# First stage of a hybrid decoder layer: loads on GpSimd's queue, stores on SP's, a fourth store tile, and a different order at both ends of the stage

## The chip, the cores and the metric

One core of a Trainium2 chip runs the kernel. Time is the device time of one execution in microseconds (us), and the figure to predict is the median of the runs. TensorE multiplies matrices (PE in the profile, PEld its weight loads), VectorE (DVE) and ScalarE (ACT) work on tiles, GpSimd (POOL) does some element-wise work and can issue DMAs, and SyncE (SP) only issues DMAs. Each of these engines takes its instructions strictly in the order in which the program gives them; a DMA issue that has to wait holds everything behind it in its engine's queue.

## The reference

```python
def reference(x, norm_gain, w_in, ret_gn_gain, w_out, final_gain):
    h = rms_norm(x, norm_gain[0])                 # x: (1, 4096, 1024) float32
    x = x + hybrid_mixer(h, w_in[0], ret_gn_gain[0], w_out[0])
    return rms_norm(x, final_gain)

def hybrid_mixer(h, w_in, ret_gn_gain, w_out):
    qa, ka, va, ga, qr, kr, vr, gr = split(h @ w_in, IN_SPLITS)   # 512 x4, 256 x2, 512 x2
    attn = dilated_attention(qa, ka, va)   # 8 heads x 64, rotary, three (window, dilation) branches
    ret = retention(qr, kr, vr)            # 4 heads, key 64, value 128, rotary, chunks of 128
    mixed = [silu(ga) * attn, silu(gr) * ret * ret_gn_gain]
    return mixed @ w_out
```

The first stage of the kernel computes the queries, keys and values: `rms_norm(x)` times the columns of `w_in` for `qa`, `ka`, `va`, `qr` and `kr`, with the rotary positions applied, and stores them in DRAM.

## The kernel before

Three stages follow each other: `phase1` (projections), `phase2` (the attention branches, the retention and `vr`'s projection), `phase3` (gates and output projection). The change is in `phase1` and in what it prepares for `phase2`.

`phase1` goes over the 4096 positions twice, in blocks q of 512 positions: q = 0 to 7 give the keys (bank 0, stored to `dr_k`) and the retention's rows (bank 1, to `dr_r`); q = 8 to 15 give the queries (`dr_q`) and the values (bank 1, `dr_v`). Every float32 product is three products of split operands (hi times hi, hi times lo, lo times hi). In place of eight 2x2 block products there are seven, P1 to P7 (`PRODUCTS`), of sums and differences of the four quarters of a block's input; each is done for two banks. So a block has 14 steps, and a step is 24 matmuls of 128x256 (L390). The quarters are the tiles `xt` (128x4x256), loaded by `load_x` (L284), changed in place by `sum_t` (L297), and split by `hi_x` (ACT, L305) and `lo_x` (DVE, L309) into `h`. Each block's sums of squares come from a second, untransposed load `xn` (`load_n`, L316; `square`, L323 on ACT; one tile for `xn` and `diag` together); `root` (L328 DVE, L330 and L332 POOL), `along_free` (PE, L341) and `copy_rb` make the row `rb` of 1/rms, with which `scale_table` (POOL, L362) scales the cosine and sine tables `tab` (`load_table`, L358).

Results leave PSUM by `snapshot` (ACT, L411 and L409) and `join` (DVE, L426 and L422) and are rotated on DVE (`rotate`, L470 to L475). Everything that is stored passes through one pool, `hlp`, tag `hl`, with three buffers: the two split key or query tiles of a half block (`hi_o` L502 or L500, `lo_o` L510 or L508, `store_o` L516), the retention's tile `or` of a half (`store_r` L484), the value tiles `vo` (`store_values`, L440 and L443 on SP and L447 on POOL).

A hand-written table sets the order: `at(step, fn, ...)` puts a function behind the matmuls of that step, with s = 14q. The final loop goes through the steps, and each engine gets its instructions in that order. Lines that matter here:

```python
hlp = pool("p1hl", 3)
at(s + 10, rotate, q, 0, 1)      # keys or queries, half 1
at(s + 12, hi_o, q, 1)
at(s + 14, store_o, q, 1)
at(s + 16, hi_o, q, 0)
at(s + 19, store_o, q, 0)
at(s + 15, rotate, q, 1, 0)      # q < 8: retention's tile "or", half 0
at(s + 17, rotate, q, 1, 1)      #        and half 1
at(s + 17, store_r, q, 0)
at(s + 18, store_r, q, 1)
at(s + 12, store_values, q, 1)   # q >= 8
```

SP issues all loads and all stores but L447. Between q = 7 and q = 8 the weights for the second pass are loaded (`load_raw`) and combined. At the end of the stage the first tiles of `phase2` are prepared: its keys (`first_k`), weights `w2` (`w2_load`, L74; `w2_split`, L83 on ACT and L84 on DVE), a chunk of x (`first_chunk`, L783; `first_chunk_split`, L792 on DVE and L795 on POOL) and queries (`first_q`, L900); the first matmuls of `phase2` are `V` (L48 to L50), of that chunk and `w2`.

Of the kernel before, what the change touches and what calls it, by code (L numbers as in the profile page):

```python
# [27 lines left out]
BLK = 512  # L28
# [110 lines left out]
def phase1(tc, io, dr, right, ahead):  # L139
# [5 lines left out]
    with ExitStack() as ctx:  # L145
# [1 line left out]
            return ctx.enter_context(tc.tile_pool(name=name, bufs=bufs, **kw))  # L147

        wp = pool("p1w", 1)
        rawp = pool("p1x", 6)  # L150
        hp = pool("p1h", 3)
        sm = pool("p1s", 2)
        tp = pool("p1t", 1)
        op = pool("p1o", 2)
        hlp = pool("p1hl", 3)
        mp = pool("p1m", 7)
        pyz = pool("p1y", 2, space=PSUM)
        pss = pool("p1ss", 1, space=PSUM)
# [14 lines left out]
        ident = wp.tile([128, 128], F32, name="ident1")  # L173
        make_identity(nc, ident)

        def whole(p, tag):
            return lambda dt: (lambda t: [t[:, k, :] for k in range(4)])(p.tile([128, 4, 512], dt, tag=tag, name=f"w1{tag}"))

        def pieces(p, tags, n):
            def get(dt):  # L180
                ts = [p.tile([128, n, 512], dt, tag=tag, name=f"w1{tag}") for tag in tags]
                return [ts[k // n][:, k % n, :] for k in range(4)]

            return get
# [33 lines left out]
            },  # L218
        )

        def load_w(ps, dst, part, k):

            rows = io["w1"][k * 128 : (k + 1) * 128, :]

            def pairs_of(c0):
                return rows[:, c0 : c0 + 512].rearrange("k (u t c) -> k t u c", t=2, c=128)[:, part]

            nc.sync.dma_start(dst[:, 0:256].rearrange("k (u c) -> k u c", c=128), pairs_of(0 if ps else 512))
            if ps == 0:
                nc.sync.dma_start(dst[:, 256:512].rearrange("k (u c) -> k u c", c=128), pairs_of(1024))  # L230
            else:
                nc.sync.dma_start(dst[:, 256:512], rows[:, 1536 + 256 * part : 1792 + 256 * part])

# [43 lines left out]
        def load_x(q, part, half, k=None):  # L277

            c0 = q % NBLK * BLK + half * HALF
            if (q, part, half) not in xq:  # L280
                xq[q, part, half] = rawp.tile([128, 4, HALF], F32, tag="x", name="xt1")
            t = xq[q, part, half]
            if k is None:
                nc.sync.dma_start(t, by_blocks(io["xT"])[:, 4 * part : 4 * part + 4, c0 : c0 + HALF])  # L284
            else:
                nc.sync.dma_start(t[:, k, :], io["xT"][(4 * part + k) * 128 : (4 * part + k + 1) * 128, c0 : c0 + HALF])

# [25 lines left out]
        def load_n(q, i):  # L313
            xn[q, i] = tp.tile([128, D], F32, tag="xn", name="xn1")
            n = 4 * q + i
            nc.sync.dma_start(xn[q, i], io["x"][n * 128 : (n + 1) * 128, :])  # L316

        def square(q, i):

# [29 lines left out]

        def load_rb(q):  # L350
            rb = rbs[q] = tp.tile([128, BLK], F32, tag="rb", name="rb1")
            nc.sync.dma_start(rb, dr["rs"][q % NBLK : q % NBLK + 1].rearrange("o i p -> o (i p)").broadcast_to([128, BLK]))

        def load_table(q, n, half):
            c0 = q % NBLK * BLK + half * HALF
            tab = tabs[q, n, half] = tp.tile([128, 2, HALF], F32, tag=f"tab{n}{half}", name="tab1")
            for i, nm in enumerate((f"cos{n}", f"sin{n}")):
                nc.sync.dma_start(tab[:, i, :], io[nm][:, c0 : c0 + HALF].unsqueeze(0).broadcast_to([4, 32, HALF]))  # L358

        def scale_table(q, n, half):  # L360
            rb = rbs[q][:, half * HALF : (half + 1) * HALF].unsqueeze(1).broadcast_to([128, 2, HALF])
# [173 lines left out]
        for q in range(NB2):  # L535
            s = STEPS * q
            one = q < NBLK
            if q:

                for n, (part, half) in zip((12, 10, 8, 5), ((0, 0), (0, 1), (1, 1), (1, 0))):  # L540
                    at(s - n, load_x, q, part, half)
                at(s - 4, hi_x, q, "P1")
                at(s - 3, lo_x, q, "P1")
                at(s - 3, sum_t, q, 1)
                at(s - 2, hi_x, q, "P5")
                at(s, lo_x, q, "P5")
                at(s, sum_t, q, 2)
                at(s + 1, hi_x, q, "P6")
                at(s + 2, lo_x, q, "P6")
            if one and q:  # L550

                a, d = {1: (-3, 2), 2: (-7, 2), 3: (-10, 2)}.get(q, (-14, 3))
                for i in range(4):
                    at(s + a + d * i, load_n, q, i)
                    at(s + a + d * i + d - 1, square, q, i)
                e = s + a + 4 * d
                at(e, root, q)
                at(e + 1, along_free, q)
                at(e + 1, copy_rb, q)
            elif not one:  # L560
                at(s - 2, load_rb, q)
# [15 lines left out]
                    at(s + max(c, {0: 10, 1: 8}.get(q, 0)), scale_table, q, n, half)  # L577

            for bank in range(2):
                at(s + 1 + 2 * bank, snapshot, q, "x", bank, "m1", 0)  # L580
                at(s + 5, snapshot, q, "z", bank, "m5", 1)
# [12 lines left out]
            if one:  # L594
                at(s + 15, rotate, q, 1, 0)
                at(s + 17, rotate, q, 1, 1)
                at(s + 17, store_r, q, 0)
                at(s + 18, store_r, q, 1)
            else:
                at(s + 12, store_values, q, 1)  # L600
                at(s + 14, last_v, q)
                at(s + 15, store_values, q, 0)

# [1 line left out]
        raw = {}  # L605

        def load_raw(name, room, part, k0):
            raw[name] = ROOM[room](F32)
            for k in range(4):
                load_w(1, raw[name][k], part, k0 + k)  # L610

        def diff_d():
            raw["D"] = ROOM["q01"](F32)
# [49 lines left out]

        def w2_load():
            ahead["w2"] = Split(nc, wpool, "w2", io["w2"], scale=gain, tag="w")
            ahead["w2"].load(mp.tile([128, 512], F32, tag="m", name="raw1"))
# [45 lines left out]
        for k in range(4):  # L712
            split_w(0, "P1", Aa, 0, ks=[k])
            hi_x(0, "P1", slice(k, k + 1))
            lo_x(0, "P1", slice(k, k + 1))
            for bank in range(2):
                product(W[0], 0, "P1", bank, [k])
        sum_t(0, 1)
        hi_x(0, "P5")
        lo_x(0, "P5")  # L720
        for k in range(4):
# [3 lines left out]
            split_w(0, "P5", Ba, ks=[k])  # L725
            for bank in range(2):
                product(W[0], 0, "P5", bank, [k])
        sum_t(0, 2)
        hi_x(0, "P6")
        lo_x(0, "P6")  # L730
# [1091 lines left out]
```

## Time and profile before

| | |
|---|---|
| runs | median 2569.85 us of 3, from 2562.11 to 2574.93 |
| the profiled execution | 2571.75 us, of which the span of the profile is 2570.0 |
| stage 1 on TensorE | from 6.63 us to the wait that ends at 916.57 |
| TensorE, 950 to 1000 us (second stage) | busy 50.00 of 50.00, clock 1.00 |
| DMA traffic, 0 to 900 us | 147.25 MB, 137.17 MB of it in SP's queue |

A row of the timeline is start, duration, engine, line, operation, tile written <- tiles read, and in brackets the idle time before it and what ended that. "SPq" is a DMA issue on SP. A row of the waits is waiting engine and line <- what it waited for: total, times, longest. A row of the windows gives, for a stretch of time, the busy time and instructions of each engine, then TensorE's granted clock, the DMA engines' share and GB/s.

### The profile page before, as it was taken

Reading aid. Unit: us, or ns where it says so; the run is one execution under the profiler, and the core shown is the slowest. Engines: PE = TensorE matmul, PEld = TensorE weight load, DVE = VectorE, ACT = ScalarE, POOL = GpSimd, SP = SyncE. Lnnn points to the kernel's source line nnn. Section 1 sums busy time; section 2 is a strip of 40 time slices with the busy share of each in tenths; the row PEclk is TensorE's granted clock in tenths of the full one; section 3 lists DMA queues with packets and bytes.
Section 4 is the critical chain, followed back from the end, with each engine's and each line's share of the span. In section 5 each row is a group of like instructions: output and inputs, shape, how many; then the busy total and the mean of one; then the engine's idle time right before and its main releaser. Section 6 shows DMA issues by size and latency. Waiting matters only on the chain. (4 is left out here: it accounts for less than half of the span.)

```text
span 2570.0 us, 47422 instructions
## 1 busy us (share of the span) xinstructions
PE 2319.0 (90%) x16808; PEld 2086.2 (81%) x16808; DVE 1758.1 (68%) x4221; ACT 1116.3 (43%) x3036; POOL 751.9 (29%) x853
## 2 busy tenths in 40 slices
PE   5768878579999659999999999999799999999998
PEld 5768778579999648888888888787688999999997
DVE  6756777686676547778787787978665656555563
ACT  5333333233232226667667666666532323222231
POOL 1211111312222235444353443544521211212110
PEclk8888988789999879999999999999899999999999
DMA  6444445446666855857658576575576556566563
GB/s 188 145 131 147 144 136 163 136 152 186 184 186 184 208 153 134 192 135 167 160 134 194 129 177 154 129 176 155 155 183 153 162 157 151 161 143 172 143 150 93
DMA packets 480174, 404.93 MB, mean 158 GB/s; under 512 B 197720, under 2 KB 444632, under 8 KB 474816
## 3 DMA queue, kind: packets, MB, share of 16 engines
q1 hardware_dynamic: 472976, 391.64, 57.7%
q0 software_dynamic: 6672, 9.99, 1.5%
q8 instruction: 133, 2.18, 0.4%
q14 instruction: 105, 0.86, 0.1%
q10 hardware_dynamic: 288, 0.26, 0.0%
HBM read 283.12 MB, written 118.64 MB: 156 GB/s over the span
## 5 line engine op out<-in xcount | busy, mean ns | idle before, releaser
L1048 DVE CUSTOM_DVE_ANT_0 S<-S,mask 128x256 f32<-128x256 f32 (+1 forms) x768 | 308.5, 402 | 165.7 <-PE S L1027 131.1
L1055 ACT ACTIVATE P<-S,nm 128x256 f32<-128x256 f32 (+1 forms) x768 | 337.9, 449 | 44.4 <-DVE nm L1048 41.5
L50 PE MATMUL g<-h,wg 128*128 128x256 f32 x1024 | 289.3, 283 | 0.0
L305 ACT ACTIVATE h<-xt 128x1024 fp32r<-128x1024 f32 (+1 forms) x115 | 118.9, 1034 | 225.8 <-DVE xt L297 99.2
L1064 PE MATMUL T<-ident,P 128*128 128x128 f32 x1368 | 214.1, 274 | 0.0
L49 PE MATMUL po<-wo,m 128*128 128x512 f32 x512 | 200.8, 392 | 0.0
L1097 PE MATMUL O<-pt,v 128*64 128x128 f32 (+1 forms) x1968 | 196.5, 326 | 0.0
L50 PEld LDWEIGHTS g<-h,wg 128*128 128x128 f32 x1024 | 195.8, 191 | 0.0
L1027 PE MATMUL S<-kk,qc 128*128 128x256 f32 x1024 | 187.4, 307 | 6.8 <-issue 2.9
L309 DVE TENSOR_TENSOR h<-xt,h 128x1024 fp32r<-128x1024 f32 (+1 forms) x115 | 155.3, 1355 | 52.1 <-ACT h L305 50.4
L48 PE MATMUL po<-wohi,m 128*128 128x512 f32 x448 | 178.7, 399 | 7.2 <-ACT m L40 6.6
L1027 PEld LDWEIGHTS S<-kk,qc 128*128 128x128 f32 x1024 | 150.1, 191 | 35.1 <-issue 17.6
L50 PE MATMUL po<-wohi,m 128*128 128x512 f32 x448 | 177.5, 397 | 0.2 <-DVE m L41 0.2
L1611 POOL TENSOR_TENSOR rs<-v,mhalf 128x1 f32<-128x1 f32 x32 | 17.6, 550 | 547.2 <-DVE v L1609 492.9
L1097 PEld LDWEIGHTS O<-pt,v 128*64 128x64 f32 x1968 | 121.4, 137 | 60.7 <-issue 31.8
L362 POOL TENSOR_TENSOR tab<-tab,rb 128x512 f32<-128x512 f32 x48 | 70.6, 1475 | 339.3 <-DMA tab<-in_sinR_dram 155.7
L1064 PEld LDWEIGHTS T<-ident,P 128*128 128x128 f32 x1368 | 164.6, 142 | 0.2 <-ACT wg0hi L87 0.2
L1550 ACT ACTIVATE e<-g 128x256 f32<-128x256 f32 x128 | 48.3, 379 | 252.9 <-PE g L50 236.4
L795 POOL TENSOR_TENSOR hc<-hr,hc 128x512 fp32r<-128x512 f32 x64 | 85.7, 1339 | 246.2 <-ACT hc L794 180.7
L1055 ACT ACTIVATION_READ_ACCUMULATOR P<-S,nm 128x1 f32 x768 | 157.5, 205 | 0.0
L48 PE MATMUL V<-w2hi,hc 128*128 128x512 f32 x256 | 118.9, 464 | 37.5 <-DVE hc L792 36.7
L49 PE MATMUL g<-h,wg1hi 128*128 128x256 f32 x512 | 145.7, 285 | 1.9 <-DVE h L843 1.8
(267 smaller groups left out, 6511.4 us busy)
## 6 DMA issues: line engine op xcount, KB each, us to landing
hr<-in_xT_dram SPq DMA_DIRECT2D x64, 512.0 KB
q<-dr_q SPq DMA_DIRECT2D x128, 256.0 KB
xt<-in_xT_dram SPq DMA_DIRECT2D x63, 512.0 KB
wb<-dr_w SPq DMA_DIRECT2D x128, 192.0 KB
o<-dr_o SPq DMA_DIRECT2D x192, 128.0 KB
v<-dr_v SPq DMA_DIRECT2D x94, 256.0 KB
xn<-in_x_dram SPq DMA_DIRECT2D x32, 512.0 KB
dr_k<-hl SPq DMA_DIRECT2D x64, 256.0 KB
```

Of the source, the lines that this page charges most:

```text
L48: nc.tensor.matmul(out, wh, xh, start=first and i == 0, stop=False)
L49: nc.tensor.matmul(out, wh, xl, start=False, stop=False)
L50: nc.tensor.matmul(out, wl, xh, start=False, stop=last and i == n - 1)
L305: nc.scalar.activation(xs[q, prod][:, 0, ks, :], xq[(q, *SOURCE[prod])][:, ks, :], AF.Copy)
L309: (engine or nc.vector).tensor_tensor(h[:, 1, ks, :], src[:, ks, :], f32(h[:, 0, ks, :]), ALU.subtract)
L362: nc.gpsimd.tensor_tensor(tabs[q, n, half], tabs[q, n, half], rb, ALU.mult)
L795: nc.gpsimd.tensor_tensor(hc[:, :, 1, :], src, hc[:, :, 0, :].bitcast(F32), ALU.subtract)
L1027: nc.tensor.matmul(s[:, j * 256 : (j + 1) * 256], qq[h, t, half][:, off : off + 128] if br == 0 else it["q"][:, t, i, :], rhs, start=(j == ...
L1048: nc.vector.tensor_tensor_reduce(sv, sv, mask[:, it["br"], c0:256], 1.0, BIG, ALU.add, ALU.min, accum_out=nm[:, col : col + 1])
L1055: nc.scalar.activation(it["P", i // 2][:, i % 2, c0:256], sv, AF.Exp, bias=nm[:, col : col + 1], scale=-1.0, accum_out=den[:, col : col + 1])
L1064: nc.tensor.transpose(t[:, j * 128 : (j + 1) * 128], it["P", bank][:, j // 2, j % 2 * 128 : j % 2 * 128 + 128], ident)
L1097: nc.tensor.matmul(o[64 * bank : 64 * bank + 64, c0 : c0 + 128 * m], vt[h, br, idx // 8][:, idx % 8, :], it["pt"][:, a : a + m, :].rearran ...
```

## The change

- `load_x` for q > 0, `load_n`, `load_table`, `load_rb` and the first keys of `phase2` are issued by GpSimd's queue; the startup's loads of x and weights, and all stores that were SP's, stay on SP.
- `hlp` gets four buffers. The six shared buffers of `xt` become five: two for the quarter (0,0), one each for the others; the order and steps in which the quarters are loaded change with it.
- `load_raw` fetches the last 256 columns of its weights in one or two DMAs in place of four.
- The squares of blocks 5 to 7 move two steps earlier; block 0's snapshots are issued right behind the products they copy, ahead of the work for the next product.
- `store_values` of half 1 moves from step s+12 to s+11. At the end, `w2` is loaded in four lots over four steps, `w2_split` and the first chunk move by one step, and `first_q` from s-4 to s.

The diff, cut to its core:

```diff
-        rawp = pool("p1x", 6)
+        rawp = pool("p1x", 1)
+        raw2p = pool("p1x2", 2)
-        hlp = pool("p1hl", 3)
+        hlp = pool("p1hl", 4)
...
             if (q, part, half) not in xq:
-                xq[q, part, half] = rawp.tile([128, 4, HALF], F32, tag="x", name="xt1")
+                p = rawp if part or half else raw2p
+                xq[q, part, half] = p.tile([128, 4, HALF], F32, tag=f"x{part}{half}", name="xt1")
             if k is None:
-                nc.sync.dma_start(t, by_blocks(io["xT"])[:, 4 * part : 4 * part + 4, c0 : c0 + HALF])
+                (nc.gpsimd if q else nc.sync).dma_start(t, by_blocks(io["xT"])[:, 4 * part : 4 * part + 4, c0 : c0 + HALF])
...
-            nc.sync.dma_start(xn[q, i], io["x"][n * 128 : (n + 1) * 128, :])
+            nc.gpsimd.dma_start(xn[q, i], io["x"][n * 128 : (n + 1) * 128, :])
...
-                nc.sync.dma_start(tab[:, i, :], io[nm][:, c0 : c0 + HALF].unsqueeze(0).broadcast_to([4, 32, HALF]))
+                nc.gpsimd.dma_start(tab[:, i, :], io[nm][:, c0 : c0 + HALF].unsqueeze(0).broadcast_to([4, 32, HALF]))
...
-                for n, (part, half) in zip((12, 10, 8, 5), ((0, 0), (0, 1), (1, 1), (1, 0))):
+                for n, (part, half) in zip((12, 10, 8, 6), ((0, 0), (1, 1), (0, 1), (1, 0))):
...
-                a, d = {1: (-3, 2), 2: (-7, 2), 3: (-10, 2)}.get(q, (-14, 3))
+                a, d = {1: (-3, 2), 2: (-7, 2), 3: (-10, 2), 4: (-14, 3)}.get(q, (-16, 3))
...
-                at(s + 12, store_values, q, 1)
+                at(s + 11, store_values, q, 1)
...
-        at(s - 12, load_raw, "Aa", "wh0", 0, 0)
+        at(s - 11, load_raw, "Aa", "wh0", 0, 0)
-        at(s - 10, load_raw, "Ab", "p40", 0, 4)
+        at(s - 8, load_raw, "Ab", "p40", 0, 4)
...
-            ahead["kk"] = load_k(nc, kka, dr, 0)
+            ahead["kk"] = load_k(nc, kka, dr, 0, nc.gpsimd.dma_start)
...
-        at(s - 6, first_chunk)
-        at(s - 4, first_q)
         for i in range(4):
-            at(s - 4 + i, w2_split, (2 * i, 2 * i + 1))
-        at(s - 1, first_chunk_split)
+            at(s - 8 + i, w2_some, (2 * i, 2 * i + 1))
+        at(s - 5, first_chunk)
+        at(s, first_q)
+        for i in range(4):
+            at(s - 3 + i, w2_split, (2 * i, 2 * i + 1))
+        at(s - 2, first_chunk_split)
...
+        for bank in range(2):
+            snapshot(0, "x", bank, "m1", 0)
```

SP's queue in block 4, before (`dr_rs` is the row of 1/rms that `copy_rb` stores; a number behind a tile's name tells one buffer's use from the next):

```order
L346 DMA dr_rs<-rb_2262 1x512
L358 DMA tab_2265<-in_cosA_dram 128x1x256
L358 DMA tab_2265<-in_sinA_dram 128x1x256
L516 DMA dr_k<-hl_2214 128x2x256 x2
L516 DMA dr_k<-hl_2215 128x2x256 x2
L316 DMA xn_2299<-in_x_dram 128x1024
L358 DMA tab_2371<-in_cosA_dram 128x1x256
L358 DMA tab_2371<-in_sinA_dram 128x1x256
L284 DMA xt_2374<-in_xT_dram 128x4x256
L484 DMA dr_r<-or_2326 4x32x256 x4
L316 DMA xn_2420<-in_x_dram 128x1024
L484 DMA dr_r<-or_2403 4x32x256 x4
```

The same stretch of SP's queue now:

```order
L353 DMA dr_rs<-rb_2267 1x512
L523 DMA dr_k<-hl_2217 128x2x256 x2
L523 DMA dr_k<-hl_2218 128x2x256 x2
L491 DMA dr_r<-or_2331 4x32x256 x4
L491 DMA dr_r<-or_2408 4x32x256 x4
L523 DMA dr_k<-hl_2371 128x2x256 x2
L523 DMA dr_k<-hl_2372 128x2x256 x2
```

The loads are gone from between the stores. They stand in POOL's queue, among its own work (L369 is `scale_table`), which before held `scale_table` and `root` alone:

```order
L323 DMA xn_2344<-in_x_dram 128x1024
L365 DMA tab_2378<-in_cosA_dram 128x1x256
L365 DMA tab_2378<-in_sinA_dram 128x1x256
L291 DMA xt_2381<-in_xT_dram 128x4x256
L369 TENSOR_TENSOR tab_2270<-tab_2270,rb_2267 128x512
L365 DMA tab_2458<-in_cosR_dram 128x1x256
L365 DMA tab_2458<-in_sinR_dram 128x1x256
L291 DMA xt_2461<-in_xT_dram 128x4x256
L323 DMA xn_2463<-in_x_dram 128x1024
L369 TENSOR_TENSOR tab_2378<-tab_2378,rb_2267 128x512
```

A multiply of a table now stands between the loads, and each table's load is four steps ahead of its multiply, as before.

The end of the stage in SP's queue, before (`w` and `raw` are the rows of `w2`, `hr` the chunk of x, `vo` the values of block 15, half 1):

```order
L74 DMA w_7956<-in_w_dram 128x512
L74 DMA raw_7943<-in_w_dram 128x512
L783 DMA hr_8017<-in_xT_dram 128x8x128
L900 DMA q_00_8081<-dr_q 32x2048 x4
L900 DMA q_10_8086<-dr_q 32x2048 x4
L440 DMA dr_v<-vo_8014 8x16x512
L443 DMA dr_v<-vo_8014 8x16x512
L440 DMA dr_v<-vo_8014 8x16x512
L443 DMA dr_v<-vo_8014 8x16x512
```

And now:

```order
L74 DMA w_8032<-in_w_dram 128x512
L74 DMA raw_7935<-in_w_dram 128x512
L807 DMA hr_8035<-in_xT_dram 128x8x128
L447 DMA dr_v<-vo_7999 8x16x512
L450 DMA dr_v<-vo_7999 8x16x512
L447 DMA dr_v<-vo_7999 8x16x512
L450 DMA dr_v<-vo_7999 8x16x512
L1746 DMA rgain_8270<-in_ret_gain_dram 128x4
L807 DMA hr_8160<-in_xT_dram 128x8x128
L523 DMA dr_q<-hl_8144 128x2x256 x2
L523 DMA dr_q<-hl_8145 128x2x256 x2
L924 DMA q_00_8209<-dr_q 32x2048 x4
```

The values' stores have changed places with the loads of the queries.

More of the change, by code (lines that the diff above doesn't have):

```diff
@@ L174, in phase1, with get @@
         make_identity(nc, ident)
+        WHOLE = {}
         def whole(p, tag):
-            return lambda dt: (lambda t: [t[:, k, :] for k in range(4)])(p.tile([128, 4, 512], dt, tag=tag, name=f"w1{tag}"))
+            def get(dt):
+                t = WHOLE[tag] = p.tile([128, 4, 512], dt, tag=tag, name=f"w1{tag}")
+                return [t[:, k, :] for k in range(4)]
+            return get
         def pieces(p, tags, n):
             def get(dt):
-                ts = [p.tile([128, n, 512], dt, tag=tag, name=f"w1{tag}") for tag in tags]
+                ts = WHOLE["h0"] = [p.tile([128, n, 512], dt, tag=tag, name=f"w1{tag}") for tag in tags]
                 return [ts[k // n][:, k % n, :] for k in range(4)]
@@ L219, in phase1, with pairs_of @@
         )
+        def pairs_of(rows, c0, part):
+            return rows[:, c0 : c0 + 512].rearrange("k (u t c) -> k t u c", t=2, c=128)[:, part]
         def load_w(ps, dst, part, k):
             rows = io["w1"][k * 128 : (k + 1) * 128, :]
-            def pairs_of(c0):
-                return rows[:, c0 : c0 + 512].rearrange("k (u t c) -> k t u c", t=2, c=128)[:, part]
-            nc.sync.dma_start(dst[:, 0:256].rearrange("k (u c) -> k u c", c=128), pairs_of(0 if ps else 512))
+            nc.sync.dma_start(dst[:, 0:256].rearrange("k (u c) -> k u c", c=128), pairs_of(rows, 0 if ps else 512, part))
             if ps == 0:
-                nc.sync.dma_start(dst[:, 256:512].rearrange("k (u c) -> k u c", c=128), pairs_of(1024))
+                nc.sync.dma_start(dst[:, 256:512].rearrange("k (u c) -> k u c", c=128), pairs_of(rows, 1024, part))
             else:
@@ L351, in load_rb @@
             rb = rbs[q] = tp.tile([128, BLK], F32, tag="rb", name="rb1")
-            nc.sync.dma_start(rb, dr["rs"][q % NBLK : q % NBLK + 1].rearrange("o i p -> o (i p)").broadcast_to([128, BLK]))
+            nc.gpsimd.dma_start(rb, dr["rs"][q % NBLK : q % NBLK + 1].rearrange("o i p -> o (i p)").broadcast_to([128, BLK]))
         def load_table(q, n, half):
@@ L579, in phase1 @@
             for bank in range(2):
-                at(s + 1 + 2 * bank, snapshot, q, "x", bank, "m1", 0)
-                at(s + 5, snapshot, q, "z", bank, "m5", 1)
+                if q:
+                    at(s + 1 + 2 * bank, snapshot, q, "x", bank, "m1", 0)
+                    at(s + 5, snapshot, q, "z", bank, "m5", 1)
                 at(s + 6 + bank, snapshot, q, "x", bank, "u2", 1)
@@ L607, in load_raw @@
         def load_raw(name, room, part, k0):
-            raw[name] = ROOM[room](F32)
+            raw[name] = t = ROOM[room](F32)
             for k in range(4):
-                load_w(1, raw[name][k], part, k0 + k)
+                rows = io["w1"][(k0 + k) * 128 : (k0 + k + 1) * 128, :]
+                nc.sync.dma_start(t[k][:, 0:256].rearrange("k (u c) -> k u c", c=128), pairs_of(rows, 0, part))
+            rows = by_blocks(io["w1"])[:, k0 : k0 + 4, 1536 + 256 * part : 1792 + 256 * part]
+            if room in ("wh0", "wh1", "p40"):
+                nc.sync.dma_start(WHOLE[room][:, :, 256:512], rows)
+            else:
+                for j, w in enumerate(WHOLE[room]):
+                    nc.sync.dma_start(w[:, :, 256:512], rows[:, 2 * j : 2 * j + 2])
         def diff_d():
@@ L665, in w2_load, with w2_some @@
             ahead["w2"] = Split(nc, wpool, "w2", io["w2"], scale=gain, tag="w")
-            ahead["w2"].load(mp.tile([128, 512], F32, tag="m", name="raw1"))
+            raw["w2"] = mp.tile([128, 512], F32, tag="m", name="raw1")
+        def w2_some(js):
+            ahead["w2"].load(raw["w2"], js)
         def w2_split(ks):
@@ L727, in phase1 @@
                 product(W[0], 0, "P5", bank, [k])
+        for bank in range(2):
+            snapshot(0, "z", bank, "m5", 1)
         sum_t(0, 2)
```

## The prediction

> **What bounds the kernel now.** I read the page first, then the time by stretches, then the waits of the first 950 us (the first stage and its end), then the order of time in one block.
>
> ```profile
> span 2570.0 us, 47422 instructions
> PE 2319.0 (90%) x16808; PEld 2086.2 (81%) x16808; DVE 1758.1 (68%) x4221; ACT 1116.3 (43%) x3036; POOL 751.9 (29%) x853
> PEclk8888988789999879999999999999899999999999
> ```
>
> PE is busy for 90%: 251 us of the span are without a matmul, and the clock row shows that the first third, where the diff is, has the low digits. Two blocks of the first half of the stage, six of the second half and a piece of the next stage, by stretches (span, then busy PE, PEld, DVE, ACT, POOL, then granted clock, DMA share and GB/s):
>
> ```profile
> 211.47:267.77 56.30, 45.60 (x338) 44.15 (x338) 37.53 (x45) 19.17 (x26) 8.29 (x6) 0.88 0.46 150
> 267.77:323.34 55.57, 43.84 (x338) 42.74 (x339) 39.82 (x47) 19.14 (x26) 8.35 (x6) 0.91 0.47 152
> 575.83:841.03 265.20, 248.33 (x2017) 246.89 (x2017) 180.14 (x229) 78.86 (x120) 67.63 (x108) 0.97 0.62 185
> ```
>
> A block of the first half takes 55.6 us; one of the second half takes 265.20/6 = 44.2, of which PE works 248.33/6 = 41.4. The same 336 matmuls of products cost 11.4 us more in the first half, though no engine is full there (DVE has 39.82 of 55.57). So waits set the pace, not work. What PE waits for, in 0 to 950 (total, times, longest):
>
> ```profile
> PE z L390 <- DVE h L309: 64.6, 12, 15.9
> PE V L48 <- DVE hc L792: 36.7, 1, 36.7
> PE x L390 <- DVE o L471: 28.1, 10, 8.0
> PE x L390 <- ACT m L411: 22.0, 3, 10.0
> ```
>
> The first is an addition of x (`lo_x`) that comes late on DVE. Who makes DVE late, with the other waits that matter:
>
> ```profile
> DVE or L471 <- DMA dr_r<-or: 77.6, 8, 16.4
> ACT xn L323 <- DMA xn<-in_x_dram: 145.8, 24, 26.5
> POOL tab L362 <- DMA tab<-in_sinR_dram: 155.7, 12, 20.2
> POOL rs_all L330 <- DVE v L328: 140.7, 8, 41.3
> ```
>
> DVE itself waits for one thing, the store of its own retention rows, eight times. In one block (start, duration, engine, line, operation):
>
> ```profile
> 278.92 4.13 SPq L484 DMA_DIRECT2D dr_r<-or  x4
> 281.68 0.68 DVE L470 TENSOR_TENSOR t<-m,tab 128x512 f32<-128x512 f32 x1
> 281.81 5.91 PE L390 MATMUL x<-h,w1q 128*128 128x256 f32 x47 [1.40 <-DVE h L309]
> 289.92 0.69 DVE L471 TENSOR_TENSOR or<-m,tab 128x512 f32<-128x512 f32 x1 [7.56 <-DMA dr_r<-or]
> 290.78 1.06 ACT L323 ACTIVATE xn<-xn 128x1024 f32<-128x1024 f32 x1 [6.55 <-DMA xn<-in_x_dram]
> 295.47 8.00 PE L390 MATMUL z<-h,w1kk 128*128 128x256 f32 x47 [7.63 <-DVE h L309]
> ```
>
> The stores are queued from 278.92, SP is held at them for 4.13 us, and DVE, which needs the tile for the second half's rows, stands for 7.56 us. The rotation and `lo_x` behind it come 7.6 us late, PE idles 7.63, and the next 47 matmuls take 8.00 where the ones before took 5.91: 2.09 us are lost to a lower clock after the pause.
>
> **Term 1, a fourth tile for stores, in the first half: −68.** The second half's rows no longer take the tile whose store is under way, but that of the key rows stored four steps earlier. So the 7.56 us wait has nothing to wait for. Eight such waits hold 77.6 us on DVE and 64.6 on PE, and each costs 2.09 of clock: 8 × 2.09 = 16.7. What PE can win is bounded by 77.6 + 16.7 = 94 above. It is not all won, because DVE has work that piles up just behind: 39.82 us per block have to fit, in order, and a `lo_x` that is on time here will wait elsewhere. I take off 1.2 a block for that: 7.56 + 2.09 − 1.2 = 8.5, times 8 is 68. At half the DVE wait, 40, is the lower end. A block then takes about 47 us, 7 above DVE's busy time, and 3 above the second half's. Next late is POOL's `diag` for the rows' roots, and the rotations that PE waits for at L471.
>
> **Term 2, the fourth tile in the second half: −10.** Here ACT, not DVE, waits for a free tile, and PE only now and then:
>
> ```profile
> ACT hl L500 <- DMA dr_q<-hl: 64.9, 7, 16.5
> ACT hl L500 <- DMA dr_v<-vo: 19.6, 2, 10.6
> 621.38 2.90 PE L390 MATMUL x<-w1kk,h 128*128 128x256 f32 x12 [3.70 <-DVE o L471]
> ```
>
> Those 84.5 us mostly go, since one tile more is free and the values leave a step sooner. But PE loses only 44.2 − 41.4 = 2.8 us a block there, 19.6 in seven blocks. Between 0 and 20 I take the middle.
>
> **Term 3, the end of the stage: −33.** PE ends the stage's products at 879.9 and starts V at 916.57:
>
> ```profile
> 879.55 11.63 SPq L900 DMA_DIRECT2D q<-dr_q  x8
> 892.76 0.63 SPq L440 DMA_DIRECT2D dr_v<-vo  x1
> 906.77 0.63 ACT L500 ACTIVATE hl<-o 128x512 fp32r<-128x512 f32 x1 [24.68 <-DMA rgain<-in_ret_gain_dram]
> 908.04 1.59 DVE L84 SCALAR_TENSOR_TENSOR w<-w,gain_all,w2hi 128x512 fp32r<-128x512 f32 x2 [21.72 <-ACT w2hi L83]
> 916.57 0.76 PE L48 MATMUL V<-w2hi,hc 128*128 128x512 f32 x1 [36.70 <-DVE hc L792]
> ```
>
> The eight loads of the first queries hold SP for 11.63 us; the last stores of values go only at 892.76; ACT stands 24.68 us at `hi_o` for the tile that they hold; behind it on ACT are the splits of `w2`, behind those DVE's, and behind DVE's the cast of the first chunk that V needs. (The load named in ACT's row is the last that SP issued; the stores before it are what holds the tile.) Afterwards the queries stand behind the values' stores, `w2` comes in lots from eight steps ahead, the keys' load is in another queue, and the cast stands ahead of the last rotation. Then V can start about 4 us after the products: 36.7 − 4 = 33. The ends are 20 (the last rotation with its 8 us on DVE still ahead of S, and the queries' load now late by its 11.63) and 41 (all of it, and the clock).
>
> **Term 4, the start: +2.**
>
> ```profile
> 10.00:15.00 5.00, 4.51 (x37) 4.31 (x36) 2.96 (x4) 2.30 (x4) 0.04 (x1) 1.00 0.95 267
> 39.08 8.28 PE L390 MATMUL x<-h,w1q 128*128 128x256 f32 x48 [10.00 <-ACT m L411]
> 50.96 4.28 PE L390 MATMUL z<-h,w1kk 128*128 128x256 f32 x21 [3.60 <-ACT m L411]
> ```
>
> One load of squares and eight of tables, 1.5 MB by the sizes in the code, no longer queue behind the weights on SP but start at once on POOL. The DMA engines are 95% busy there at 267 GB/s, so 1.5 MB pushes the first weights back by at most 5.6 to 5.9 us. The earlier copies of `x` and `z` (snapshots) take the 3.60 away and perhaps a part of the 10.00: +5.6 − 3.6 = +2, with −10 and +6 as ends.
>
> **Term 5, loads that POOL issues: +8.** About 200 loads of the stage leave SP, 16 in each first-half block (four of x, four of squares, eight halves of tables). The nearest rows for their price are the stores that POOL issues already, and the loads of squares on SP:
>
> ```profile
> L447 POOL DMA_DIRECT2D dr_v<-vo x128 | 69.6, 551 | 188.6 <-DVE vo L525 102.4 <-DVE vo L422 84.5 <-DMA rq<-dr_r 1.7
> DMA to landing us min/median/max: 3.5/6.1/10.3
> 260.12 0.34 SPq L316 DMA_DIRECT2D xn<-in_x_dram  x1
> 263.48 1.06 ACT L323 ACTIVATE xn<-xn 128x1024 f32<-128x1024 f32 x1 [2.43 <-DMA xn<-in_x_dram]
> ```
>
> A POOL issue costs 0.55 us of POOL: 16 × 0.55 = 8.8 us on an engine with 8.35 of 55.57 busy, so it fits. Landing takes 6.1 us by the stores' row, 3.4 (263.48 − 260.12) by SP's: each load lands 2.7 later, if the row of stores holds for loads. x is asked for six to twelve steps ahead (18 us and more), so that costs nothing. The squares are one piece of work on ACT, in order, ahead of copies that PE waits for; ACT has 19.14 of 55.57 busy and covers most, so I count 1 us a block. POOL runs in order too: behind its waits for tables (155.7) and for the root's sum (140.7) now stand loads. Each table's load is four steps, some 12 us, ahead of its multiply, about the same as those waits. On the other side SP's queue gets free of 200 loads, and stores go at once; this is in terms 1 and 2. Ends: −10 and +50.
>
> What the stores' row cannot tell is whether DVE suffers when POOL writes descriptors:
>
> ```profile
> 276.62 1.67 DVE L473 TENSOR_TENSOR m<-m,tab 128x512 f32<-128x512 f32 x1
> 291.25 0.69 DVE L473 TENSOR_TENSOR m<-m,tab 128x512 f32<-128x512 f32 x1
> 799.88 4.31 POOL L447 DMA_DIRECT2D dr_v<-vo  x8 [14.26 <-DVE vo L525]
> 799.90 1.21 DVE L309 TENSOR_TENSOR h<-xt,h 128x1024 fp32r<-128x1024 f32 x1
> ```
>
> DVE's product took 1.67 instead of 0.69 when it overlapped a POOL multiply, so these two engines do hold each other up; but during eight stores issued by POOL, an addition took its usual 1.21. I count nothing for it, and keep the other as a rival.
>
> The Trainium skill, "SBUF — State Buffer", section "SBUF: two separate sides", speaks against the change: a DMA issued from GpSimd has its descriptors written by GpSimd's own cores, and a VectorE operation in a two-port mode keeps them out, so that the transfer starts late; it advises the queues of SP or ACT. By that rule the loads land later by the DVE operation that they meet. The row of landings, 6.1 against 3.4, agrees with a delay and not with its cause, and with a delay of one DVE operation more, 1.2 us for each of the four squares of a block, the sum would be 8 × 4.8 = 38 us higher. The skill's "DMA: Bandwidth & Descriptors", section "Issuing engines are not separate DMA queues", says that issuing from several engines saves no more than the issue time, usually small; by it the queue move would be worth nothing, as I have it.
>
> **Term 6, second-pass weights in lots: −4.** Four lots of eight DMAs become five or six, eleven issues fewer on SP at about 0.4 us (the row of 260.12 has 0.34). DVE is fully busy where these weights are combined, so 0 to −8.
>
> **Sum.** −68 − 10 − 33 + 2 + 8 − 4 = −105. The profiled execution took 2571.75 us (span 2570.0), 1.9 over the median 2569.85. 2571.75 − 105 = 2466.75, less 1.9: 2465.
>
> **The rivals.** 0.5% (12.8 us) is about what a measurement of this kernel can tell from no change.
>
> *Squares late on POOL.* Loads behind POOL's waits make ACT's wait at L323 longer instead of shorter, and since ACT copies for PE in order, PE follows. For it: 145.8 us of that wait today. Against it: much of today's comes from SP's queue, which this loses. At 1.5 us more for four squares in seven blocks, 42 us: −105 + 42 = −63, about 2507.
>
> *The wait only changes its owner.* The fourth tile is taken at once by something else, and `or` still waits for a store. Against it: the order has the key rows' store four steps before. Term 1 is then 0: −37, 2533.
>
> *More than counted.* First-half blocks reach the second half's 44.2: 8 × 11.4 = 91 instead of 68, and the start gains a little: 2440.
>
> *Slower: POOL's loads slow DVE.* If each load that POOL issues held DVE as its multiply does, by 1.67 − 0.69 = 0.98 us, then 128 loads in eight first-half blocks cost 125 us of DVE, and DVE at 39.82 + 15.7 = 55.5 would be the bound at today's pace: −105 + 125 = +20, 2590. It decides from 105/128 = 0.82 us per load. Against it: the addition of 1.21 at 799.90.
>
> *No change*, if POOL's waits eat what the tiles give: 2570.
>
> **How the numbers follow.** The main case 0.60, with 2430 to 2490 as its own range (term 1 between 94 and 40, the others at their ends in part); squares late 0.16; changed owner 0.06; more 0.08; slower 0.06; no change 0.04. The range 2425 to 2530 holds the main case but for a tail, "more" but for a tail, and the late squares, and leaves out the changed owner, the slower case and no change with 0.16. Faster by over 0.5%: 0.60 + 0.16 + 0.06 + 0.08 = 0.90; within: 0.04; slower: 0.06.
>
> **What would show it.** Right: DVE at L471 waits for no store (under 10 us in all), first-half blocks of 45 to 49 us with a clock over 0.93, ACT's waits for stores under 30 us in the second half, V within 10 us of the last product, landings of POOL's loads at 5 to 7 us with DVE's rotation and additions unchanged in length. Wrong: ACT's wait for squares over 200 us, table multiplies that PE's rotations wait for, DVE's 0.69 rows at over 1 us near POOL's issues, or a start of the stage (to the first product of the second block) that is over 10 us longer.

## The result, and the profile after

The changed kernel takes 2459.91 us (median of four runs, 2458.83 to 2460.55), the kernel before 2570.09 on the same chip: a ratio of 0.9574, interval 0.9549 to 0.9598, or 110 us less. That is 5 us from the forecast of 2465 and inside the main case. The terms behind it were not right, though: four were far too small or too large, and one had the wrong sign. The errors cancel.

The page of the profile after:

```profile
span 2458.7 us, 47420 instructions
PE 2306.5 (94%) x16808; PEld 2072.8 (84%) x16808; DVE 1757.4 (71%) x4221; ACT 1115.2 (45%) x3036; POOL 903.1 (37%) x1053
PEclk8899999799999899999999999999999999999999
```

Work is unchanged on DVE and ACT, POOL carries 151 us more (200 instructions more: the loads that it now issues), and the span is 111.3 us shorter. PE's busy time falls by 12.5 of these with the same matmuls: the clock row is higher in its first third.

Where the time went, by stretches (span, then busy PE, PEld, DVE, ACT, POOL, granted clock, DMA share, GB/s). The five rows are the start with block 0, blocks 1 to 7, block 8 (where the weights of the second half are made), blocks 9 to 15, and the pause before V. Before:

```profile
0.00:77.24 77.24, 50.70 (x338) 47.85 (x339) 53.08 (x67) 38.03 (x60) 15.39 (x16) 0.85 0.58 170
77.24:497.40 420.16, 319.95 (x2368) 309.60 (x2367) 275.61 (x333) 143.94 (x196) 64.54 (x46) 0.87 0.47 149
497.40:570.43 73.03, 50.01 (x339) 48.93 (x338) 64.37 (x76) 26.09 (x40) 24.68 (x19) 0.81 0.40 123
570.43:879.87 309.44, 289.04 (x2354) 287.02 (x2352) 206.63 (x262) 91.27 (x140) 83.59 (x135) 0.98 0.65 188
879.87:916.57 36.70, 0.00 (x1) 0.03 (x1) 14.45 (x29) 5.29 (x9) 2.99 (x4) 0.56 0.58 140
```

After:

```profile
0.00:90.65 90.65, 58.48 (x338) 53.28 (x339) 53.17 (x68) 39.09 (x61) 26.98 (x33) 0.85 0.57 145
90.65:435.68 345.03, 306.91 (x2369) 298.35 (x2367) 279.29 (x329) 140.89 (x194) 156.94 (x159) 0.95 0.59 182
435.68:507.74 72.06, 48.91 (x339) 48.13 (x338) 68.14 (x83) 29.13 (x43) 26.50 (x29) 0.81 0.41 124
507.74:788.36 280.62, 280.62 (x2354) 280.42 (x2352) 199.64 (x260) 95.54 (x146) 122.95 (x189) 1.00 0.70 213
788.36:793.20 4.84, 0.01 (x2) 0.04 (x1) 4.67 (x12) 0.00 (x0) 1.71 (x4) 1.00 0.45 151
```

So the start lost 13.4 us, blocks 1 to 7 won 75.1, block 8 won 1.0, blocks 9 to 15 won 28.8 and the pause 31.9. What comes after V's start took 2570.0 − 916.57 = 1653.4 before and 2458.7 − 793.20 = 1665.5 now: 12.1 lost. The sum is −111.3. In blocks 9 to 15 PE has no idle time left: 40.1 us a block at a clock of 1.00.

Waits in 0 to 950 us (total, times, longest):

```profile
ACT xn L330 <- DMA xn<-in_x_dram: 104.2, 25, 8.8
POOL xt L291 <- DVE h L316: 105.9, 19, 22.3
POOL xn L323 <- ACT xn L330: 85.7, 20, 8.0
POOL tab L369 <- DMA tab<-in_sinA_dram: 16.4, 7, 4.7
PE rb L348 <- POOL diag L339: 16.1, 7, 4.2
```

DVE's wait for the store of the retention rows at their rotation (77.6 before) has no row any more, and ACT's waits for the stores of queries and values fall from 84.5 to 4.7. ACT waits less for squares (145.8 before), and POOL's table multiplies hardly wait for their loads (155.7 for one of the four tables alone before); instead POOL waits at the issue of a load until its tile is free: that of x by DVE, that of the squares by ACT. Lines are seven higher at the rotation and in the loads than before (L471 is L478).

### The profile page after: what moved, and what is told of

Same layout as the page of the kernel before. It is cut to its first block, busy times and chain, and to the rows that moved or that the text cites. A ratio compares the mean times of both kernels' runs of the same rounds, so it can differ in the third digit from the quotient of the medians.

```text
span 2458.7 us, 47420 instructions
## 1 busy us (share of the span) xinstructions
PE 2306.5 (94%) x16808; PEld 2072.8 (84%) x16808; DVE 1757.4 (71%) x4221; ACT 1115.2 (45%) x3036; POOL 903.1 (37%) x1053
## 3 DMA queue, kind: packets, MB, share of 16 engines
q0 software_dynamic: 34576, 75.16, 10.5%
## 4 chain that ended last, share of the span: by engine, by line
PE 68%; DMA 5%; DVE 5%; issue 2%; ACT 1%; SPq 1%; POOL 1%; POOLq 0%; DVEq 0%; ACTq 0%
PE S L1051 8%; PE x L397 7%; PE O L1121 7%; PE T L1088 5%; PE po L48 4%; PE po L50 4%; PE po L49 4%; PE g L50 4%; PE g L49 4%; PE g L48 4%; PE z L397 3%; PE V L48 2%; PE V L50 2%; PE V L49 2%; PE y L397 2%
## 5 line engine op out<-in xcount | busy, mean ns | idle before, releaser
L40 ACT ACTIVATE m<-e 128x256 fp32r<-128x256 f32 x128 | 53.1, 417 | 214.0 <-DVE e L1581 129.7
L49 PE MATMUL g<-h,wg1hi 128*128 128x256 f32 x512 | 146.6, 287 | 2.8 <-DVE h L867 2.5
L48 PE MATMUL g<-h,wg1hi 128*128 128x256 f32 x512 | 145.2, 285 | 4.1 <-ACT e L1574 3.4
```

The lines of the kernel that those rows point to most:

```text
L48: nc.tensor.matmul(out, wh, xh, start=first and i == 0, stop=False)
L49: nc.tensor.matmul(out, wh, xl, start=False, stop=False)
```

## The experiments

The pause at a store could have been ended by the tile or by moving the loads out of SP's queue. **Tile theory:** the retention rows of the second half need a tile, and the fourth gives it. **Queue theory:** stores and loads stand in each other's way on SP, and the move to POOL's queue gives the gain. The first four runs tell them apart.

**The tile alone**, in the kernel before:

```diff
-        hlp = pool("p1hl", 3)
+        hlp = pool("p1hl", 4)
```

(with the x tiles and their order of loading as in the diff, which make its room).

> The kernel before with the fourth tile for stores alone (and the x tiles in the changed kernel's five, which make its room; loads stay in SP's queue, the end and the start of the stage as before). Tile theory (the wait was for a tile): first-half blocks of 46 to 50 us, DVE waits at the rotation for a store under 10 us, second-half blocks 40 to 42; 2570 - 75 - 20 = about 2475. Queue theory (stores landed late because loads stood between them on SP, and the move of the loads brought the gain): blocks stay above 53, time over 2540.

Measured: 2485.68 us, ratio 0.9683 (0.9663 to 0.9703). The first two rows are blocks 1 to 7 and 9 to 15; the waits are those of 77 to 465 us, of POOL, PE and SP:

```profile
77.37:464.28 386.91, 311.38 (x2368) 301.25 (x2367) 275.02 (x332) 142.15 (x196) 66.56 (x45) 0.90 0.51 162
534.34:814.97 280.63, 280.63 (x2354) 280.42 (x2352) 202.34 (x260) 91.34 (x139) 82.72 (x131) 1.00 0.69 207
POOL tab L364 <- DMA tab<-in_sinR_dram: 120.5, 12, 15.5
POOL tab L364 <- DMA tab<-in_sinA_dram: 69.4, 9, 9.7
PE rb L343 <- POOL diag L334: 36.7, 6, 7.7
SPq L318 <- ACT xn L325: 72.5, 12, 14.0
SPq L348 <- ACT rb L347: 64.7, 7, 11.0
```

The second half has its whole gain from the tile. Blocks 1 to 7 have 33 of 75; they take 51 to 67 us each, not 46 to 50. The wait for the store is gone, and with it 60 of the 64 us for which PE stood at a late `lo_x` in these blocks. Other waits of PE take part of that back. The wait for POOL's `diag` at the roots, up to 7.7 us a time, was there before and is now twice as long. Both before, 77 to 497 us:

```profile
PE z L390 <- DVE h L309: 60.4, 8, 15.9
PE rb L341 <- POOL diag L332: 18.5, 6, 5.3
```

ACT's copies and a late `join` take 18 us more. The rows of POOL and SP above give the chain of `diag` backwards. `diag` stands in POOL's queue behind table multiplies and behind the sum of the squares; the multiplies wait 190 us for tables; tables and squares are loaded by SP; and SP stands 72.5 us at a load of squares until ACT frees the one tile, and 64.7 at the store of the roots until ACT has copied them. Whatever stands behind in SP's queue comes late. It can land late too. Two loads of squares, each issue followed by the square on ACT that waited for it:

```profile
285.83 1.55 SPq L318 DMA_DIRECT2D xn<-in_x_dram  x1
294.71 1.06 ACT L325 ACTIVATE xn<-xn 128x1024 f32<-128x1024 f32 x1 [14.80 <-DMA xn<-in_x_dram]
295.89 0.34 SPq L318 DMA_DIRECT2D xn<-in_x_dram  x1
299.41 1.06 ACT L325 ACTIVATE xn<-xn 128x1024 f32<-128x1024 f32 x1 [2.60 <-DMA xn<-in_x_dram]
```

The first, right behind four stores and three other loads, takes 8.9 us; the second, issued after SP had stood for 6.7 us, takes 3.5. ACT waited for 26 of the 27 loads of squares in blocks 1 to 7, until a median of 7.2 us after their issue. Tile theory has the cause of the old wait, but less than half of the first half's gain.

**Three tiles in the changed kernel** (the same line back).

> The changed kernel with three tiles for stores again. Tile theory: the wait at the rotation for a store comes back with 5 us or more a block, first-half blocks above 52 us, second half at 43 or more: 2460 + 60 to 90 = 2520 to 2550. Queue theory: with the loads gone from SP's queue the stores land in time with three tiles too: under 2480.

Measured: 2530.26, ratio 0.9852 (0.9837 to 0.9866): 70 slower than the changed kernel. The wait is back (140 to 430 us):

```profile
DVE or L478 <- DMA dr_r<-or: 38.3, 5, 13.4
```

**The loads back on SP in the changed kernel**, all other steps as changed:

```diff
-                (nc.gpsimd if q else nc.sync).dma_start(t, by_blocks(io["xT"])...
+                nc.sync.dma_start(t, by_blocks(io["xT"])...
-            nc.gpsimd.dma_start(xn[q, i], ...
+            nc.sync.dma_start(xn[q, i], ...
```

(and the same for `rb` and the tables).

> The changed kernel with the loads of x, squares, tables and roots back in SP's queue, all steps as changed. Tile theory: the queue hardly matters: 2460 within 15, and about 10 us of the first block come back. Queue theory: first-half blocks above 52 us, 2510 or more. A third way: SP's waits of each issue for the one eight before hold the stores again, and second-half blocks go above 42: 2475 to 2490.

Measured: 2486.45, ratio 0.9681 (0.9666 to 0.9696). Blocks 1 to 7 take 382.6 us; the second half keeps its 40.1. The theories share the gain: the queue is worth about as much as the tile in the first half, and nothing more in the second once the tile is there. Here PE stands longest for ACT's copies, against 8.4 us in the changed kernel (140 to 430 us):

```profile
ACT xn L330 <- DMA xn<-in_x_dram: 121.4, 19, 20.9
PE x L397 <- ACT m L418: 33.4, 5, 14.1
```

ACT does its work in order, and stands at the squares' loads ahead of its copies (80.8 us in the changed kernel).

**The first block's loads of squares and tables back on SP**, behind the weights (`nc.sync` for `q` = 0).

> The changed kernel with the loads of squares and tables of the first block alone back in SP's queue, behind the weights. Theory that the early 1.5 MB push the first weights back (SP's first weight issue after x stands at 13.45 us instead of 7.64): block 0 shrinks by 8 to 13 us, 2447 to 2452. Rival (block 0 is longer for the earlier copies or something else): 2460 within 3.

Measured: 2454.52, ratio 0.9555 (0.954 to 0.957). The start up to block 1 takes 80.1 us; in the profiled runs of the five kernels here that keep the changed start it is 86.4 to 90.7, the changed kernel's own 90.65 being the longest. So the early loads cost 6 to 10.5 us, of which the whole time shows 5.4. The rows show why the start suffered: SP's first weight after x, then the stretch 10 to 20 us, first before and then after:

```profile
7.64 0.51 SPq L228 DMA_DIRECT2D w1hc<-in_w_dram  x1
10.00:20.00 10.00, 5.31 (x39) 4.81 (x38) 6.11 (x6) 3.54 (x6) 4.23 (x3) 0.85 0.92 257
```

```profile
13.45 0.37 SPq L234 DMA_DIRECT2D w1hc<-in_w_dram  x1
10.00:20.00 10.00, 5.77 (x23) 5.01 (x23) 1.64 (x3) 2.11 (x4) 0.00 (x0) 1.00 1.16 169
```

The DMA engines' share is higher, and they move 169 GB/s instead of 257. With the tables alone early and the squares behind the weights (the second kernel of the next pair) the start still takes 88.2 us, with this row for 10 to 20 us:

```profile
10.00:20.00 10.00, 6.05 (x23) 4.99 (x23) 3.44 (x7) 3.19 (x6) 0.00 (x0) 1.00 1.15 222
```

So the eight early tables, 1 MB, cost some 8 us, where their bytes at 257 GB/s would be 4.

**Which of the loads?** Squares alone on POOL (from block 1), x, tables and roots on SP; and the reverse, squares alone on SP.

> The changed kernel with the loads of x, tables and roots in SP's queue, and of the moved loads only the squares' (from the second block on) issued by POOL. Squares theory: with the loads on SP, PE waits for POOL's diag or for ACT's copies, because the squares' load stands behind stores in SP's queue and ACT stands at it (longest 20.9 us against 8.8); then this kernel has first-half blocks 1 to 7 in 345 to 355 us together and 2448 to 2456 in all (block 0 as with the start on SP). Rival (the loads of x or of tables are what profits from POOL): blocks 1 to 7 stay near 383, 2480 or more.

> The changed kernel with the squares' loads alone back in SP's queue, x, tables and roots on POOL. Squares theory: blocks 1 to 7 back to 370 to 385 us, 2485 to 2500. Rival (x and tables gone from SP, SP is free enough for the squares to be in time): 345 to 350, 2460 within 5. Between the two: the squares' load is late only by what stands ahead of it, and both count.

Measured: 2465.3, ratio 0.9593 (0.9576 to 0.9609), blocks 1 to 7 in 365.6; and 2464.46, ratio 0.9582 (0.9565 to 0.96), in 352.6. All on SP is 382.6, all on POOL 345.0. So the squares' theory, that they alone matter, fell: their own move gives 17 of 38, the others' move gives 30, and in the first of the two kernels PE waited 40.1 us for `diag`, which stood behind multiplies whose tables came late from SP. Each kind of load gains by leaving SP's queue.

Why it gains is only in part settled. Three things change with the move, and no run changes one of them alone. Loads no longer stand behind SP's waits. SP issues less: in blocks 1 to 7 its issues take 220 us in sum with the tile alone, and 122 with tile and queue (a kernel below). And a square on ACT that waits for its load starts 5.5 us after the load's issue there (median), in place of 7.2. For the first speaks that SP's waits remain and the gain comes all the same. With tile and queue SP stands 122.1 us at the store of the roots (77 to 470 us), where it was 64.7 with the tile alone, but behind it now stand only stores and the loads of weights:

```profile
SPq L353 <- ACT rb L352: 122.1, 7, 22.6
```

**The end of the stage as before**, in the changed kernel: `w2` in one step, keys by SP, queries four steps ahead, the chunk a step sooner, its cast a step later.

```diff
-        at(s - 5, first_chunk)
-        at(s, first_q)
+        at(s - 6, first_chunk)
+        at(s - 4, first_q)
-            at(s - 3 + i, w2_split, (2 * i, 2 * i + 1))
-        at(s - 2, first_chunk_split)
+            at(s - 4 + i, w2_split, (2 * i, 2 * i + 1))
+        at(s - 1, first_chunk_split)
```

> The changed kernel with the end of the stage as before: second weight w2 loaded in one step and split a step sooner, keys loaded by SP, queries four steps ahead of the end, the chunk of x a step sooner and its cast a step later. Theory that the fourth tile alone freed the end (with the tile alone the pause before V was 12.2 and not 36.7, and from the last product to the end of the kernel 1669.8, against 1670.4 here): 2460 within 4. The prediction's view (the order is what brings 33): 2480 or more.

Measured: 2448.04, ratio 0.9526 (0.9512 to 0.954), 12 us faster than the changed kernel; in the profiled runs 10.0 of it lie behind the last product (1660.4 against 1670.4). Neither view was right: the new order is not idle, it costs. With the tile alone, the time from the last product to the end was already 1669.8 (1690.1 before, 1670.4 in the changed kernel), with a pause of 12.2 in front of V. So with four tiles the new order isn't needed. With three it does help: the kernel with three tiles above, which has the new order, has a pause of 7.7, and with three tiles and the old order (the last kernel below) it is 29.8.

**`w2` two steps sooner**, to bring the scores forward.

> The changed kernel with the loads and the splits of w2 two steps sooner and the chunk of x one. Now the first scores (S) come 24.9 us after V starts, where before it was 14.8. Theory that V's matmuls wait for w2's splits on DVE, which stand behind the last rotation (2.85 us at L84, 1.0 at L1421): S comes 5 to 10 us sooner, 2450 to 2456. Rival (they wait for the low parts of the chunk on POOL and run at a low clock after the pause in any order): 2460 within 3. Loss: the earlier w2 loads hold SP ahead of the stores of queries, and the last blocks lengthen.

Measured: 2457.46, ratio 0.9559 (0.9545 to 0.9573). From the last product to the end 1669.4: nothing gained there. The splits were not what the scores waited for.

**The queries' loads alone four steps ahead again**, the rest of the end as changed:

```diff
-        at(s, first_q)
+        at(s - 4, first_q)
```

> The changed kernel with the first queries' loads four steps ahead of the stage's end again, ahead of the values' stores, and the rest of its end as changed. Theory that the late queries are what makes the changed end 12 us worse (their eight loads now stand at 800.9 us in SP's queue, ahead of the last values' stores and the next chunk's load at 818.75, at which ACT waits 24.8): 2448 to 2452. Rival (w2's later splits or the keys on POOL): 2457 or more. The prediction's step (eight loads ahead of the stores hold ACT for a tile and V with it): V starts 20 us or more later, 2475 or more.

Measured: 2447.83, ratio 0.9521 (0.9502 to 0.954), as fast as with the whole end undone. In the profiled runs 7.1 us of the gain lie behind the last product (1663.3 against 1670.4) and 4.3 in the start, which isn't changed and varies as told above. So the late queries are 7 of the end's 10 us at least, and the other 3 aren't told apart. In the changed kernel (SP's loads of the queries and of the next chunk of x, ACT's copy of that chunk, PE's scores):

```profile
800.92 6.88 SPq L924 DMA_DIRECT2D q<-dr_q  x8
818.75 0.37 SPq L807 DMA_DIRECT2D hr<-in_xT_dram  x1
829.52 0.63 ACT L818 ACTIVATE hc<-hr 128x512 fp32r<-128x512 f32 x1 [24.83 <-DMA hr<-in_xT_dram]
831.01 1.22 PE L1051 MATMUL S<-kk,q 128*128 128x256 f32 x4 [7.89 <-ACT P L1079]
```

and with the queries early:

```profile
811.57 0.59 SPq L807 DMA_DIRECT2D hr<-in_xT_dram  x1
816.29 0.63 ACT L818 ACTIVATE hc<-hr 128x512 fp32r<-128x512 f32 x1 [16.10 <-DMA hr<-in_xT_dram]
```

Late queries make the next chunk's load late in SP's queue; ACT stands at its copy, the probabilities `P` behind it on ACT come late, and PE waits 7.89 us for them. With the queries early PE has no such wait. V starts 4.83 us after the last product in both.

**The start and the end undone together**, and then **the tile and the queue alone**, everything else as before (squares' steps, the first block's copies, the values' step, the weights not in lots).

> The changed kernel with two parts undone: the first block's loads of squares and tables back on SP behind the weights (worth 5 by the run with that alone), and the end of the stage as before (worth 12 by that run). If the two add: 2443, between 2438 and 2448. If the end's gain was that run's own: 2454.

> The kernel before with the fourth tile (and the x tiles and their order) and the loads of x, squares, tables and roots in POOL's queue from the second block on; all else as before: the steps of the squares, the first block's copies, the values' store a step later, the weights not in lots, the end. Theory that tile and queue are the whole gain: within 5 of the kernel with the start and the end undone, about 2440 to 2450. Rival, that the sooner squares are part of it (with a late load of squares PE waits 7.5 us a block for POOL's diag): blocks 2 to 6 lose 3 us or more each, 2458 or more.

Measured: 2442.38, ratio 0.9501 (0.9481 to 0.9522): the two add, 5 and 12 by the medians. And 2436.76, ratio 0.9487 (0.947 to 0.9505), the fastest of all; its interval lies clear of the changed kernel's and overlaps the other's. Its blocks 1 to 7, and what PE waits for `diag` there (77 to 418 us):

```profile
76.96:417.96 341.00, 303.28 (x2368) 294.53 (x2367) 281.13 (x331) 140.97 (x194) 156.56 (x159) 0.95 0.61 185
PE rb L348 <- POOL diag L339: 16.2, 6, 4.3
```

The sooner squares are no part of the gain; the rival fell.

**The queue alone**, the fourth corner: the kernel just told, with three tiles.

> The kernel before with the loads of x, squares, tables and roots in POOL's queue from the second block on and the x tiles and their order alone; three tiles for stores, all else as before. With the kernel before (2569), the tile alone (2486) and both (2437) this is the fourth corner. If the two are independent, the queue is worth 49 without the tile too: 2520. If a wait for a store costs the same wherever the loads are, as with three tiles in the changed kernel (70 slower): 2507. If the queue helps only when the tile is there (DVE's wait for the store hides the late squares): 2550 or more.

Measured: 2520.83, ratio 0.981 (0.9787 to 0.9833). Blocks 1 to 7, and DVE's wait in 0 to 950:

```profile
76.89:459.06 382.17, 309.86 (x2369) 300.00 (x2367) 283.22 (x331) 142.06 (x194) 158.07 (x159) 0.92 0.55 165
DVE or L478 <- DMA dr_r<-or: 56.3, 8, 13.8
```

The four corners: neither 2569, tile 2486 (−83), queue 2521 (−48 or −49), both 2437 (−132). In the whole time the two add up, but by stretches they don't. In blocks 1 to 7 both together win 79.2, 8 more than the tile (33.3) and the queue (38.0) by themselves; in blocks 9 to 15 the queue by itself wins 11.2, and beside the tile nothing. The two differences cancel. Nor is the way the same. With three tiles the queue's move makes DVE wait less for stores (56.3 in place of 77.6); with four it makes PE wait less in blocks 1 to 7 for `diag` (36.7 to 16.2) and for ACT's copies (22.7 to 7.5).

The x tiles and their order are the same in the last three corners, and were not run alone. With them the same, the tile is worth 84 (2521 to 2437) and the queue 49 (2486 to 2437); so, as far as such sums tell, little of the gain is theirs. The changed kernel's other parts together cost it 23 us: 2437 against 2460.

## Why the prediction was right in its number, and where its steps were not

**Term 1 (−68 for the tile in the first half).** The mechanism was right: the wait for the store belonged to the tile, and goes with it and comes back with it. The size was off: the tile alone gives 33 in blocks 1 to 7. I took off 1.2 us a block for waits that DVE would find elsewhere, and bounded PE's gain by DVE's 77.6 instead of PE's own waits. PE's waits for `lo_x` fell by 60 in blocks 1 to 7, but its waits for `diag`, for ACT's copies and for a join grew by 36, half of it `diag`, which the prediction named as next late without pricing it. What is left is 25 us of idle time and 9 of busy time.

**Term 2 (−10).** It measured −28.8, outside its bound of 19.6. That bound counted PE's idle time alone and took the 41.4 busy us a block as fixed. At a clock of 1.00 the same matmuls need 40.1, so the clock was 1.2 us a block of the 4.1 won (289.04 against 280.62 in seven blocks), and the idle time went wholly, where I took half. The tile alone does it; the values' store a step sooner brings nothing that the runs can tell (it is undone in the fastest kernel, with the same 40.1).

**Term 3 (−33).** The pause shrank by 31.9, as forecast, but with four tiles it takes no new order for that: with tile and queue and the old order it is 6.2. What counts is the time from the last product to the end, which fell by 20 only, since the new order costs 10 there, 7 of them by the late queries. I had them in the bounds ("the queries' load now late by its 11.63") and not in the value. With three tiles the order does help, as the prediction reasoned: 1682.2 with the queue alone and the old end, 1669.8 with three tiles and the new one. A remedy for a wait turned into a cost when another remedy had removed the wait.

**Term 4 (+2).** 13.4 in the profiled run, 9 to 13 over the kernels with this start, beyond its upper end of 6. The mechanism of the early loads held, the price did not: I priced the early loads by their bytes at 267 GB/s, and in that stretch the engines moved 169. The gain booked for the first block's earlier copies was a loss. The kernel with start and end undone takes 80.1 for its start and the one with tile and queue alone 77.0, and up to there the two differ in these copies only. PE's waits for them do shrink (14.4 us to 4.0), but PE is busy for 55.9 us in place of 50.6; why is open.

**Term 5 (+8 for loads on POOL).** Wrong in sign: the queue's move is worth 49 us, far beyond the lower end of −10. I priced later landings, and said of SP's freed queue that it was "in terms 1 and 2". That is the step that failed. Stores were not the only ones to gain: the loads themselves came late in SP's queue, and through tables, roots and squares they set PE's pace as soon as the tile's wait was gone. Nor are landings from POOL's queue later. Its row for the squares has a median of 5.1 us:

```profile
L323 POOL DMA_DIRECT2D xn<-in_x_dram x32: 528/565/776, 1.5 to 369.7; - x32
DMA to landing us min/median/max: 3.5/5.1/9.2
```

The 3.4 of SP's that the prediction used belong to a load that was issued after SP had stood for 7.9 us. In blocks 1 to 7 of the kernel before, ACT waited for 22 of the 27 loads of squares on SP, until a median of 7.5 us after their issue; with tile and queue it waited for 23, until 5.5 after POOL's issue.

The Trainium skill's rule that was weighed there ("SBUF — State Buffer", section "SBUF: two separate sides") would have the loads from POOL land late; the squares landed sooner here, and no run shows a delay that VectorE causes. The Trainium skill's other rule ("DMA: Bandwidth & Descriptors", section "Issuing engines are not separate DMA queues") would have the move save issue time alone, usually little. The measurement decides: it is 49 us here, of which no run tells how much is SP's issue time, how much its waits for other engines, at which every load behind stood too, and how much the landings.

**Term 6 (−4).** Block 8 won 1.0 us, and 3.0 with the tile alone and no lots: no gain of the lots is seen.

**The sum.** Terms 1 and 5 together were −60; blocks 1 to 7, where both act, gave −75. Terms 2 and 3 gave −29 and −20 where −10 and −33 stood, and the start lost 9 to 13 instead of 2. The number is right because the errors were of both signs, and the case of late squares, with a chance of 0.16 and a price of 42, was the opposite of what happened: the same chain ran late before the change, and the move eased it.

**The slower rival** (POOL's issues hold DVE) is not what the trace shows. Its own example, the product with a table, before and after (busy, mean ns):

```profile
L473 DVE TENSOR_TENSOR m<-m,tab 128x512 f32<-128x512 f32 x48 | 37.2, 774 | 1.7
```

```profile
L480 DVE TENSOR_TENSOR m<-m,tab 128x512 f32<-128x512 f32 x48 | 35.2, 733 | 1.7
```

DVE's whole busy time is 1757.4 against 1758.1, with 200 more instructions on POOL. Of the other signs that were named, these came as said: blocks 3 to 7 at 45.5 to 49.3 us at a clock of 0.96, V 4.8 us after the last product, ACT's waits for stores, and POOL's landings. Blocks 1 and 2 took 54.7 and 53.9. And one of the signs of being wrong came: the start is 13.4 us longer, where over 10 was named.

## What to carry to other kernels

A queue that issues loads and stores in order stands at whichever waits for another engine, and the loads behind it are late without any row that says so: read who stands at the queue's waits, follow the loads behind them to the engine that needs them, and take the landings from several rows of the busy queue, before pricing a move of loads. When a wait is removed, price the waits that are next late with their own rows; here they took back more than half. Remedies for one wait should be run one at a time: of the parts of this change two brought 132 us and the rest gave 23 back.

## What the runs showed of the hardware that was not expected

Early loads of 1.5 MB by POOL cost 6 to 10.5 us of the start (86.4 to 90.7 against 80.1), where their bytes at the rate seen before would be about 6; with the 1 MB of tables alone it is 88.2. The DMA share stood at 1.16 while 169 GB/s moved, against 257 GB/s at 0.92. Of two loads of squares of the same size on SP, one was read 8.9 us after its issue, behind a run of other issues, and one 3.5 us after it, when SP had stood for 6.7. And idle time costs twice: when every wait of the second half had gone, the clock went from 0.98 to 1.00 and the busy time of the same 2354 matmuls from 289.04 to 280.62 us.
